# Four more of a gate stage's products come ahead of its second half, first pairs' weights are prepared on VectorE, and later pairs' sums queue behind the last operand

## The chip, the cores and the metric

One core of one Trainium2 chip runs the kernel. The metric is device time in microseconds (us), the median of three runs: 1529.71 us before the change (1528.55 to 1529.90). The page and the trace come from one more, profiled execution of the same program, which took 1530.54 us; its span from the first to the last instruction is 1528.7 us.

## The reference

One layer of a streaming encoder on 1024 tokens of width 1024, all in float32. The input is normalised and multiplied by `w_in` (1024 x 4256), whose columns hold a gated convolution (three times 512), the latents of an attention (384, 256 and 32) and two gates of 1024 columns each. After the attention and the output projection come an up-projection to 2 x 2816 columns, a width-3 convolution, gelu times value, a down-projection and a small gated embedding.

```
z = u @ w_in[i]
a_b, a_c, a_x, q_lat, kv_lat, k_rope, gate_a, gate_b = jnp.split(z, split_pts, axis=-1)
...
mixed = jax.nn.sigmoid(gate_a) * ya + jax.nn.sigmoid(gate_b) * yb
...
up = _causal_dwconv3(u2 @ w_ffn_up[i], conv_ffn_w[i]) + b_ffn_conv[i]
```

## The kernel before

**Products.** Every float32 matrix is held as a pair of parts, hi (ScalarE's cast, line 182) and lo (source minus hi, line 183, mostly VectorE or GpSimd), and a product of two matrices is three passes of four 128x512 matmuls: 12 matmuls (`prod`, line 306). Activations lie as eight 128x1024 tiles `u[0..7]`; the two 512-token halves are h = 0 and h = 1.

**Pairs.** Two 128-column blocks of a weight matrix are taken together. Their 2x2 block product is made with seven products instead of eight (`pair`): A11·B11, A12·B21, S2·T2, S3·T3, S1·T1, A22·T4, S4·B22. B11 and B21 come from half 0 of the activations (`first`), B22, T2, T3, T1 and T4 need half 1 as well (`second`, `third`; differences on VectorE over 128x2048, line 281, each operand then cast and split). S1 to S4 are sums and differences of the four weight blocks, made in `weights`: loads r1 and r0, the split of A22 (`who[1]`), a22 = a21 + a22 (line 336, `who[2]`), a21 = a11 - a21 (line 337, `who[3]`), and on VectorE lines 338 and 339 and two 128x1024 splits, S3 with S1 and S2 with S4. `who` is VectorE for the first and GpSimd for the other three by default. Evictions from PSUM are VectorE's lines 362, 365, 366, 375, 376, 377 and 381.

**First rows.** The products of A11 and A12 need half 0 alone. `first_row` loads a pair's first weight block a second time, splits it on VectorE and makes these two products ahead of time; ScalarE copies them out as m1 and d11 (lines 319, 324). The pair itself then has five products, its weights skip the split of A11 and A12 (`early`), and GpSimd adds m1 to d11 (line 364).

**The two places.** In the gate stage (column pairs 0 to 7 of the two gates) pairs 0 to 5 have first rows, made while half 1 is still being normalised; pairs 0 and 1 are spilled to DRAM (`d_z`) and reloaded when their turn comes, and pairs 6 and 7, made late in the stage ahead of the attention, have none. In the up-projection 12 of 22 pairs have first rows; the first pair in `order` has none, and its weights are all GpSimd's: `up_weights` passes `(G, G, G, G)`. In the down-projection, which the change does not touch, the first weights are VectorE's already.

**What sets the order.** A scheduler orders each engine's queue from the written program and its dependencies. `tc.issue_after(i)` puts the instructions written inside it behind `i` where they are on the engine of `i`, and does nothing to those on other engines. Each engine, and SyncE's DMA queue SP, works in order. Slots (s7, s8, s42, s43 for raw weights) are handed on when their last reader is done. TensorE's PSUM banks come from a ring of six in the gate stage and of four in the up-projection.

## Time and profile before

| | |
|---|---|
| median of three runs | 1529.71 us (1528.55 to 1529.90) |
| profiled execution | 1530.54 us, span 1528.7 us |
| TensorE busy | 1472.8 us (96%), mean granted clock 0.987 |
| VectorE busy | 1179.2 us (77%) |
| ScalarE busy | 698.6 us (46%) |
| GpSimd busy | 524.0 us (34%) |
| DMA | 195.56 MB, mean 128 GB/s |

The shares are averages over stages. TensorE is at 20.00 us of each 20 us window in most of the span; what is left are a few stretches in which it is not, and these are where a gain can lie. PE is TensorE, DVE VectorE, ACT ScalarE, POOL GpSimd, SP SyncE's queue.

### The profile page before, as it was taken

The page shows a single profiled execution, that of the slowest core. Times are in us where ns is not written, and L with a number is a line of the kernel's source. Part 1 is how long each engine was busy: PE and PEld are TensorE (multiplying, and loading weights), DVE is VectorE, ACT ScalarE, POOL GpSimd, SP SyncE. Part 2 cuts the span into 40 slices and gives each one's busy share as a digit, 9 for nine tenths or more (in the row PEclk, how much of TensorE's full clock was granted, in tenths as well). Part 3 has the DMA queues.
Part 4 walks back from the last instruction along what each step waited for, and adds up shares of the span by engine and source line. Part 5 has one row for each costly group of instructions (what it writes and reads, how often), then busy time and mean ns, then how long its engine had stood idle before and what let it go on. Part 6 is the DMA issues. An engine that isn't in the chain of part 4 may idle for free. (4 is left out here: it accounts for less than half of the span.)

```text
span 1528.7 us, 19246 instructions
## 1 busy us (share of the span) xinstructions
PE 1472.8 (96%) x6980; PEld 1226.6 (80%) x6980; DVE 1179.2 (77%) x1649; ACT 698.6 (46%) x1096; POOL 524.0 (34%) x388
## 2 busy tenths in 40 slices
PE   8989999999989999999997999999999999999896
PEld 6768888888768888888886888888888888787796
DVE  6898566665658888752668888999888889978886
ACT  8634222335447777443454434443434634334333
POOL 1424222215533443441127233344221021333953
PEclk9999999999999999999998999999999999999898
DMA  9325221335761012541380323433334552333432
GB/s 342 129 101 200 90 83 56 124 111 188 261 188 40 27 56 84 193 138 51 121 305 28 104 95 120 129 124 110 112 120 165 186 175 69 124 118 110 138 104 97
DMA packets 73503, 195.56 MB, mean 128 GB/s; under 512 B 7360, under 2 KB 22208, under 8 KB 73408
## 3 DMA queue, kind: packets, MB, share of 16 engines
q1 hardware_dynamic: 65056, 169.90, 34.2%
q10 hardware_dynamic: 8352, 24.44, 4.2%
q8 instruction: 55, 0.90, 0.3%
q14 instruction: 40, 0.33, 0.1%
HBM read 142.79 MB, written 51.51 MB: 127 GB/s over the span
## 5 line engine op out<-in xcount | busy, mean ns | idle before, releaser
L306 PE MATMUL psum<-s,s 128*128 128x512 f32 x3948 | 907.4, 391 | 18.5 <-DVE s L183 14.2
L306 PEld LDWEIGHTS psum<-s,s 128*128 128x128 f32 x3948 | 742.3, 189 | 178.3 <-DVE s L183 17.7
L182 ACT CAST s<-s 128x1024 fp32r<-128x1024 f32 (+3 forms) x419 | 337.3, 828 | 400.5 <-PE psum L306 137.9
L217 PE MATMUL psum<-s,s 128*128 128x512 f32 (+1 forms) x1920 | 416.6, 375 | 17.2 <-ACT s L182 11.5
L183 POOL TENSOR_TENSOR s<-s,s 128x512 fp32r<-128x512 f32 (+2 forms) x150 | 225.8, 1517 | 544.8 <-PE psum L306 352.5
L217 PEld LDWEIGHTS psum<-s,s 128*128 128x128 f32 x1920 | 336.5, 191 | 81.3 <-ACT s L182 14.0
L183 DVE TENSOR_TENSOR s<-s,s 128x1024 fp32r<-128x1024 f32 (+2 forms) x269 | 327.9, 1238 | 52.9 <-ACT s L182 43.2
L535 DVE SCALAR_TENSOR_TENSOR psum<-s,vecs,psum 128x1023 f32<-128x1023 f32 x88 | 111.7, 1279 | 2.5 <-ACT psum L533 1.5
L533 ACT ACTIVATE psum<-s,vecs 128x1024 f32<-128x1024 f32 x44 | 53.2, 1209 | 101.9 <-DVE s L377 88.1
L183 DVE TENSOR_TENSOR s<-psum,s 128x512 fp32r<-128x512 f32 (+3 forms) x144 | 70.8, 504 | 26.9 <-ACT s L182 25.8
L364 POOL TENSOR_TENSOR s<-s 128x512 f32<-128x512 f32 x22 | 33.5, 1523 | 158.1 <-DVE s L322 72.8
L182 ACT CAST s<-psum 128x512 fp32r<-128x512 f32 (+3 forms) x144 | 61.2, 445 | 38.5 <-DVE s L183 13.9
L753 PE MATMUL psum<-s,s 128*128 128x512 f32 (+2 forms) x288 | 67.4, 360 | 2.3 <-ACT s L764 2.1
L250 ACT ACTIVATE s<-s 128x512 f32<-128x512 f32 (+1 forms) x68 | 38.9, 581 | 63.5 <-DVE s L1061 29.9
L766 POOL TENSOR_SCALAR s<-s,ri 128x384 f32<-128x384 f32 (+5 forms) x48 | 41.4, 864 | 70.2 <-DVE ri L765 55.5
L337 POOL TENSOR_TENSOR s<-s,s 128x512 f32<-128x512 f32 x39 | 56.8, 1456 | 2.9
L253 DVE TENSOR_TENSOR s<-s,s 128x512 f32<-128x512 f32 (+1 forms) x55 | 46.0, 837 | 15.2 <-ACT s L250 13.6
L375 DVE TENSOR_TENSOR s<-s,psum 128x512 f32<-128x512 f32 x47 | 32.1, 682 | 31.5 <-PE psum L306 31.4
L336 POOL TENSOR_TENSOR s<-s 128x512 f32<-128x512 f32 x39 | 54.9, 1408 | 2.9
L778 PE MATMUL psum<-s,s 128*128 128x256 f32 x320 | 54.1, 292 | 1.5 <-DVE s L183 0.7
L753 PEld LDWEIGHTS psum<-s,s 128*128 128x128 f32 x288 | 46.4, 189 | 9.9 <-ACT s L764 5.3
L764 ACT ACTIVATE s<-psum,nm 128x128 f32<-128x128 f32 (+3 forms) x64 | 47.6, 746 | 14.3 <-DVE nm L762 9.0
(120 smaller groups left out, 1159.3 us busy)
## 6 DMA issues: line engine op xcount, KB each, us to landing
s<-in_w_up_dram SPq DMA_DIRECT2D x56, 512.0 KB, 3.7
s<-in_w_in_dram SPq DMA_DIRECT2D x40, 512.0 KB, 4.2
s<-in_w_down_dram SPq DMA_DIRECT2D x36, 512.0 KB, 3.7
d_f<-s SPq DMA_DIRECT2D x22, 512.0 KB, 2.6
s<-in_x_dram SPq DMA_DIRECT2D x32, 256.0 KB, 5.4
d_sg<-s ACTq DMA_DIRECT2D x16, 512.0 KB, 3.1
s<-d_sg SPq DMA_DIRECT2D x16, 512.0 KB, 4.3
s<-d_f SPq DMA_DIRECT2D x16, 512.0 KB, 6.7
```

The source lines that it names most:

```text
L182: A.copy(hi, src)
L183: last.append((eng or V).tensor_sub(lo, src, f(hi)))
L217: nc.tensor.matmul(out_ps, w[c // HALF][pw][:, c % HALF : c % HALF + P], X[k][half][px][:, cs], start=start and a == 0 and k == 0, stop=st ...
L253: V.tensor_add(acc, acc, sq)
L306: nc.tensor.matmul(pt, w[pw][:, k * P : (k + 1) * P], blk[k][px], start=a == 0 and k == 0, stop=a == 2 and k == 3,)
L336: who[2].tensor_add(a22, a21, a22)
L337: who[3].tensor_sub(a21, a11, a21)
L533: A.activation(dst, src, AF.Identity, bias=bias, scale=w2)
L535: V.scalar_tensor_tensor(dst[:, i:], src[:, : S - i], w, dst[:, i:], op0=ALU.mult, op1=ALU.add)
L753: nc.tensor.matmul(st_[:, lo_ : lo_ + w_], q[part_q][:, o : o + P], parts(K[hd, kh])[part_k][:, 0:w_], start=part_q == 0 and part_k == 0, ...
L764: A.activation(pr[:, 0:n], st_[:, 0:n], AF.Exp, bias=nm, accum_out=sm)
L778: nc.tensor.matmul(po[:, 0:256], vt[:, kt, :], t_[:, kk * 256 : (kk + 1) * 256], start=kt == 0 and part == 0, stop=kt == 2 * b + 1 and par ...
```

## The change

Pairs 6 and 7 of the gates get first rows too, made after those of pairs 0 and 1; all four are spilled and reloaded. The first pair of the gate stage (now named pair 2 in both versions) has all of its weight work on VectorE, as has the first pair of the up-projection, where `third` now also waits in the queue for that pair's last split. The weights of later pairs (for the gates: pairs 3, 4 and 5) are written inside `issue_after(behind)`, where `behind` is the last split of T4 on VectorE, so that their VectorE sums stand behind it. GpSimd's addition of m1 to d11 is put behind the same pair's a21, where GpSimd makes that.

```diff
@@ x_blocks / third
                 operand("T4", 4, 0)
+            return ends["T4"].ins
@@ weights
-        who[3].tensor_sub(a21, a11, a21)
+        w["S3 made"] = who[3].tensor_sub(a21, a11, a21)
@@ pair
-            G.tensor_add(d11, d11, m1)
+            with tc.issue_after(w["S3 made"].ins):
+                G.tensor_add(d11, d11, m1)
@@ the gate stage
-    def gate_weights(i, early=False):
-        return weights(w_in[17 + 2 * i], w_in[18 + 2 * i], raws, early)
+    def gate_weights(i, early=False, who=(V, G, G, G)):
+        return weights(w_in[17 + 2 * i], w_in[18 + 2 * i], raws, early, who)
...
-    early, spilled = [47, 48, 45, 49], 2
-    NE = len(early) + spilled
-    for i in range(NE):
-        o = f32(early[(i - NE) % len(early)])
+    early, spilled = [47, 48, 45, 49], (0, 1, 6, 7)
+    for n, i in enumerate([*spilled, *range(2, 6)]):
+        o = f32(early[n % 4])
         first_row(w_in[17 + 2 * i], B, raws, mm, o[:, hs(0)], o[:, hs(1)])
-        if i < spilled:
+        if i in spilled:
             nc.sync.dma_start(d_z[i], o)
     second()
-    w = gate_weights(spilled, True)
-    third(w)
+    w = gate_weights(2, True, (V, V, V, V))
+    behind = third(w)
     others = Ring([44, 46])
...
+    def spilled_pair(i, o, hooks=()):
+        nc.sync.dma_start(f32(o), d_z[i])
+        gate_pair(i, o, others(), True, hooks)
+
+    for n, i in enumerate(range(2, 6)):
+        if n:
+            with tc.issue_after(behind):
+                w = gate_weights(i, True)
+        gate_pair(i, early[n], others(), True, w=w)
+    for i in range(2):
+        spilled_pair(i, early[i])
...
-    for i in range(NE, 8):
-        gate_pair(i, outs(), outs(), hooks=(mixer_in, mixer_load) if i == 7 else ())
+    others = outs
+    for i in (6, 7):
+        spilled_pair(i, outs(), (mixer_in, mixer_load) if i == 7 else ())
@@ the up-projection
-        return weights(w_up[j], w_up[NFF + j], raws, j in rows, (G, G, G, G))
+        return weights(w_up[j], w_up[NFF + j], raws, j in rows, (G, G, G, G) if j != order[0] else (V, V, V, V))
...
-    third()
+    behind = third(w)
...
-        now = up(j, up_weights(j))
+        with tc.issue_after(behind):
+            w = up_weights(j)
+        now = up(j, w)
```

Lines of `weights` and `pair` move by one or two: 336 to 339 become 337 to 340, 362 and 364 to 366 become 363 and 366 to 368.

**VectorE, gate stage, from the second 128x2048 difference on.** Tiles: s38 and s34 are the activations, s17 is B22, s21 T2, s25 T3, s29 T1 and the s38 with the highest number T4; s7, s8, s42 and s43 are raw weights; other numbers are weight parts. Before (pair 2's weights are s42 and s43, pair 3's are s7 and s8):

```order
L281 TENSOR_TENSOR s38_96<-s34_102,s38_96 128x4x512
L339 TENSOR_TENSOR s42_90<-s42_90 128x512
L183 TENSOR_TENSOR s2_134<-s43_91,s1_127 128x1024
L281 TENSOR_TENSOR s34_102<-s34_102,s38_96 128x4x512
L183 TENSOR_TENSOR s0_124<-s42_90,s6_422 128x1024
L281 TENSOR_TENSOR s34_102<-s34_102 128x4x512
L183 TENSOR_TENSOR s21_119<-s34_102,s21_119 128x2x512
L338 TENSOR_TENSOR s7_88<-s8_89,s7_88 128x512
L183 TENSOR_TENSOR s21_119<-s34_102,s21_119 128x2x512
L183 TENSOR_TENSOR s25_564<-s38_96,s25_564 128x2x512 x2
L183 TENSOR_TENSOR s29_569<-s38_96,s29_569 128x2x512 x2
L339 TENSOR_TENSOR s7_88<-s7_88 128x512
```

Now (pair 2's weights are s7 and s8; the first row is the split of pair 5's first row, the second that of pair 2's A22):

```order
L183 TENSOR_TENSOR s1_127<-s43_91,s0_124 128x1024
L183 TENSOR_TENSOR s2_134<-s8_89,s2_134 128x512
L281 TENSOR_TENSOR s34_102<-s34_102,s38_96 128x4x512
L337 TENSOR_TENSOR s8_89<-s8_89 128x512
L281 TENSOR_TENSOR s34_102<-s34_102 128x4x512
L338 TENSOR_TENSOR s8_89<-s7_88,s8_89 128x512
L183 TENSOR_TENSOR s21_119<-s34_102,s21_119 128x2x512 x2
L339 TENSOR_TENSOR s7_88<-s8_89,s7_88 128x512
L183 TENSOR_TENSOR s4_390<-s8_89,s50_358 128x1024
L183 TENSOR_TENSOR s25_624<-s38_96,s25_624 128x2x512 x2
L183 TENSOR_TENSOR s29_629<-s38_96,s29_629 128x2x512 x2
L340 TENSOR_TENSOR s7_88<-s7_88 128x512
```

Pair 3's sums (lines 338 and 339 on s7) are gone from among the operands; they now follow T4. Pair 2's A22 and lines 337 and 338, which were GpSimd's, stand on VectorE between the differences. Pair 2's split of S3 with S1 has moved from among the differences to just ahead of T3, and that of S2 with S4 (the fifth row before) to behind T4. Three rows ahead of the piece stands the split of pair 4's first row, the second of the two splits that are new here.

**TensorE, gate stage, end of the first rows.** s9 is B11 and s13 B21. Before:

```order
L306 MATMUL psum_69<-s13_188,s50_357 128x512 x4
L306 MATMUL psum_69<-s13_188,s4_389 128x512 x4
L306 MATMUL psum_69<-s13_188,s50_357 128x512 x4
L306 MATMUL psum_69<-s25_564,s1_127 128x512 x4
L306 MATMUL psum_69<-s25_564,s2_134 128x512 x4
L306 MATMUL psum_69<-s29_569,s1_127 128x512 x4
L306 MATMUL psum_69<-s29_569,s2_134 128x512 x4
L306 MATMUL psum_69<-s21_119,s6_422 128x512 x2
L306 MATMUL psum_69<-s17_539,s6_422 128x512 x2
```

Now, after the row that stands third above in both versions:

```order
L307 MATMUL psum_69<-s9_183,s0_124 128x512 x4
L307 MATMUL psum_69<-s9_183,s1_127 128x512 x4
L307 MATMUL psum_69<-s9_183,s0_124 128x512 x4
L307 MATMUL psum_69<-s13_188,s0_124 128x512 x4
L307 MATMUL psum_69<-s13_188,s1_127 128x512 x4
L307 MATMUL psum_69<-s13_188,s0_124 128x512 x4
L307 MATMUL psum_69<-s25_624,s50_358 128x512 x4
L307 MATMUL psum_69<-s25_624,s4_390 128x512 x4
L307 MATMUL psum_69<-s25_624,s50_358 128x512 x4
```

In all, 48 matmuls on s9 and s13 have come in ahead of the first T3 product, and that product is made in one go, with T3's lo part in its third row; T1, T4 and only then T2 follow it.

**VectorE, up-projection, from the split of B22 on.** The first pair's weights are s42 and s43. Before:

```order
L183 TENSOR_TENSOR s17_539<-s34_102,s17_539 128x2x512 x2
L281 TENSOR_TENSOR s38_2477<-s34_102,s38_2477 128x4x512
L281 TENSOR_TENSOR s34_102<-s34_102,s38_2477 128x4x512
L338 TENSOR_TENSOR s42_4890<-s43_4891,s42_4890 128x512
L281 TENSOR_TENSOR s34_102<-s34_102 128x4x512
L339 TENSOR_TENSOR s42_4890<-s42_4890 128x512
L183 TENSOR_TENSOR s21_119<-s34_102,s21_119 128x2x512 x2
L183 TENSOR_TENSOR s25_564<-s38_2477,s25_564 128x2x512 x2
L183 TENSOR_TENSOR s29_569<-s38_2477,s29_569 128x2x512 x2
L183 TENSOR_TENSOR s0_124<-s43_4891,s6_422 128x1024
L183 TENSOR_TENSOR s50_5859<-s42_4890,s45_5858 128x1024
L183 TENSOR_TENSOR s38_6238<-s34_102,s38_6238 128x2x512 x2
```

Now:

```order
L281 TENSOR_TENSOR s38_2485<-s34_102,s38_2485 128x4x512
L337 TENSOR_TENSOR s43_4899<-s43_4899 128x512
L281 TENSOR_TENSOR s34_102<-s34_102,s38_2485 128x4x512
L338 TENSOR_TENSOR s43_4899<-s42_4898,s43_4899 128x512
L281 TENSOR_TENSOR s34_102<-s34_102 128x4x512
L339 TENSOR_TENSOR s42_4898<-s43_4899,s42_4898 128x512
L183 TENSOR_TENSOR s21_119<-s34_102,s21_119 128x2x512 x2
L340 TENSOR_TENSOR s42_4898<-s42_4898 128x512
L183 TENSOR_TENSOR s0_124<-s43_4899,s6_422 128x1024
L183 TENSOR_TENSOR s25_624<-s38_2485,s25_624 128x2x512 x2
L183 TENSOR_TENSOR s29_629<-s38_2485,s29_629 128x2x512 x2
L183 TENSOR_TENSOR s50_5867<-s42_4898,s45_5866 128x1024
```

The first pair's lines 337 and 338 are VectorE's now, and so are the splits of its A22 and of A11 with A12, which stand just above the piece; the split of S3 with S1 stands ahead of T3, not behind T1.

## Rows read from the trace of the kernel before

**Rows 1.** Part 1 of the page: busy time, share of the span and instructions of TensorE and VectorE.

```profile
PE 1472.8 (96%) x6980; PEld 1226.6 (80%) x6980; DVE 1179.2 (77%) x1649; ACT 698.6 (46%) x1096; POOL 524.0 (34%) x388
```

**Rows 2.** Windows of 20 us at the gate stage: from:to and its length, then busy time (and count) of PE, weight loads, DVE, ACT and POOL, granted clock, DMA share, GB/s.

```profile
60.00:80.00 20.00, 17.90 (x76) 13.56 (x75) 20.00 (x11) 10.85 (x16) 11.13 (x6) 1.00 0.19 52
80.00:100.00 20.00, 15.46 (x53) 11.13 (x54) 17.41 (x21) 6.90 (x9) 6.17 (x3) 0.83 0.18 57
100.00:120.00 20.00, 20.00 (x90) 16.57 (x89) 19.59 (x39) 6.14 (x9) 5.28 (x4) 1.00 0.55 206
```

**Rows 3.** The same columns at the start of the up-projection.

```profile
820.00:840.00 20.00, 10.90 (x44) 8.22 (x43) 19.34 (x12) 7.02 (x9) 12.47 (x7) 0.82 0.03 6
840.00:860.00 20.00, 20.00 (x83) 16.34 (x82) 17.43 (x21) 6.44 (x7) 6.28 (x4) 0.92 0.28 100
860.00:880.00 20.00, 20.00 (x90) 16.57 (x89) 16.85 (x19) 10.11 (x11) 3.89 (x3) 1.00 0.39 129
```

**Rows 4.** Timeline of TensorE, gate stage: start, length, line, operation, count, and in brackets the idle time ahead and what ended it.

```profile
46.96 28.37 PE L306 MATMUL psum<-s,s 128*128 128x512 f32 x123
76.96 2.47 PE L306 MATMUL psum<-s,s 128*128 128x512 f32 x8 [1.63 <-DVE s L183]
...
85.40 1.22 PE L306 MATMUL psum<-s,s 128*128 128x512 f32 x2 [1.49 <-DVE s L183]
87.78 210.88 PE L306 MATMUL psum<-s,s 128*128 128x512 f32 x920 [1.16 <-DVE s L365]
```

**Rows 5.** Timeline of VectorE, gate stage, same columns.

```profile
52.59 2.03 DVE L183 TENSOR_TENSOR s<-s,s 128x1024 fp32r<-128x1024 f32 x1
54.54 2.28 DVE L281 TENSOR_TENSOR s<-s 128x2048 f32<-128x2048 f32 x1
56.74 0.68 DVE L338 TENSOR_TENSOR s<-s,s 128x512 f32<-128x512 f32 x1
57.35 2.35 DVE L183 TENSOR_TENSOR s<-s,s 128x1024 fp32r<-128x1024 f32 x2
59.62 3.38 DVE L281 TENSOR_TENSOR s<-s,s 128x2048 f32<-128x2048 f32 x1
62.92 1.78 DVE L339 TENSOR_TENSOR s<-s 128x512 f32<-128x512 f32 x1
...
77.43 7.92 DVE L183 TENSOR_TENSOR s<-s,s 128x1024 fp32r<-128x1024 f32 x5
85.27 1.77 DVE L339 TENSOR_TENSOR s<-s 128x512 f32<-128x512 f32 x1
```

**Rows 6.** Timeline of GpSimd, gate stage: the first and the last two of the ten instructions that start between 52 and 87 us.

```profile
52.24 1.29 POOL L364 TENSOR_TENSOR s<-s 128x512 f32<-128x512 f32 x1 [0.92 <-ACT s L324]
...
82.12 2.14 POOL L336 TENSOR_TENSOR s<-s 128x512 f32<-128x512 f32 x1
84.34 2.14 POOL L337 TENSOR_TENSOR s<-s,s 128x512 f32<-128x512 f32 x1
```

**Rows 7.** Timeline of TensorE, start of the up-projection.

```profile
795.98 31.33 PE L306 MATMUL psum<-s,s 128*128 128x512 f32 x137
827.94 2.20 PE L306 MATMUL psum<-s,s 128*128 128x512 f32 x8 [0.64 <-ACT s L319]
838.60 61.58 PE L306 MATMUL psum<-s,s 128*128 128x512 f32 x261 [8.46 <-DVE s L183]
```

**Rows 8.** Timeline of VectorE, start of the up-projection.

```profile
803.41 1.22 DVE L183 TENSOR_TENSOR s<-s,s 128x1024 fp32r<-128x1024 f32 x1
804.55 2.29 DVE L281 TENSOR_TENSOR s<-s 128x2048 f32<-128x2048 f32 x1
806.75 2.36 DVE L183 TENSOR_TENSOR s<-s,s 128x1024 fp32r<-128x1024 f32 x2
809.02 5.59 DVE L281 TENSOR_TENSOR s<-s,s 128x2048 f32<-128x2048 f32 x2
820.65 1.77 DVE L338 TENSOR_TENSOR s<-s,s 128x512 f32<-128x512 f32 x1 [6.04 <-POOL s L337]
822.35 3.37 DVE L281 TENSOR_TENSOR s<-s 128x2048 f32<-128x2048 f32 x1
...
826.25 15.71 DVE L183 TENSOR_TENSOR s<-s,s 128x1024 fp32r<-128x1024 f32 x10
```

**Rows 9.** Timeline of GpSimd, start of the up-projection.

```profile
804.86 12.02 POOL L183 TENSOR_TENSOR s<-s,s 128x512 fp32r<-128x512 f32 x2 [19.63 <-PE psum L306]
816.83 1.30 POOL L336 TENSOR_TENSOR s<-s 128x512 f32<-128x512 f32 x1
818.07 1.30 POOL L364 TENSOR_TENSOR s<-s 128x512 f32<-128x512 f32 x1
819.33 1.29 POOL L337 TENSOR_TENSOR s<-s,s 128x512 f32<-128x512 f32 x1
...
828.48 2.38 POOL L183 TENSOR_TENSOR s<-s,s 128x512 fp32r<-128x512 f32 x1 [4.91 <-ACT s L182]
```

**Rows 10.** Windows of 20 us, columns as in rows 2, ahead of the attention.

```profile
400.00:420.00 20.00, 17.80 (x79) 14.42 (x78) 12.14 (x19) 5.76 (x15) 7.65 (x6) 1.00 0.83 255
420.00:440.00 20.00, 17.54 (x71) 14.04 (x71) 7.84 (x15) 5.06 (x11) 3.53 (x3) 0.92 0.89 269
```

**Rows 11.** Part 6 of the page: DMA issues, count, KB each, median us from issue to landing.

```profile
s<-in_w_in_dram SPq DMA_DIRECT2D x40, 512.0 KB, 4.2
```

More of the change, by code (lines that the diff above doesn't have):

```diff
@@ L458, in gate_pair @@
             A.dma_start(d_sg[2 * i + j], f32(o_))
-    early, spilled = [47, 48, 45, 49], 2
-    NE = len(early) + spilled
-    for i in range(NE):
-        o = f32(early[(i - NE) % len(early)])
+    early, spilled = [47, 48, 45, 49], (0, 1, 6, 7)
+    for n, i in enumerate([*spilled, *range(2, 6)]):
+        o = f32(early[n % 4])
         first_row(w_in[17 + 2 * i], B, raws, mm, o[:, hs(0)], o[:, hs(1)])
-        if i < spilled:
+        if i in spilled:
             nc.sync.dma_start(d_z[i], o)
     second()
-    w = gate_weights(spilled, True)
-    third(w)
+    w = gate_weights(2, True, (V, V, V, V))
+    behind = third(w)
     others = Ring([44, 46])
-    for n, i in enumerate([*range(spilled, NE), *range(spilled)]):
-        o = early[n % len(early)]
-        if n >= len(early):
-            nc.sync.dma_start(f32(o), d_z[i])
-        gate_pair(i, o, others(), True, w=w if n == 0 else None)
+    def spilled_pair(i, o, hooks=()):
[8 more added lines that the diff above has]
+        spilled_pair(i, early[i])
     def rotary_tables():
```

## The prediction, as put on record before the run

> **What bounds the kernel now.** I read the busy times first: TensorE works 1472.8 us of a span of 1528.7 [rows 1], so at most some 56 us can be had anywhere, and only where TensorE waits. Then the 20 us windows: nearly all show TensorE at 20.00 with 90 matmuls of 128x512, which is 20/90 = 0.222 us a matmul. Two places that the change touches do not. In the gate stage two windows hold 76 and 53 matmuls, 51 short of 180, so 51 x 0.222 = **11.3 us** are lost there [rows 2]. At the start of the up-projection two windows hold 44 and 83, 53 short, so **11.8 us** [rows 3]. In both the granted clock falls after the waits (0.83; 0.82, then 0.92), so part of the time ran at 1.2 GHz and not at 2.4; the matmul counts have that in them.
>
> Next, the timeline of TensorE for what ends the waits. In the gate stage it runs without a gap from 46.96 us for 123 matmuls, then stops and starts until 87.78 us, and VectorE's line 183, the splits, ends the waits [rows 4]. In the up-projection there is one wait of 8.46 us, ended by the same line [rows 7]. Then VectorE itself: from 52.59 to 87 us in the gate stage it has no idle time, 20.00 of 20 in one window [rows 2, 5]; in the up-projection it is busy too, but for 6.04 us in which its line 338 waits for GpSimd's line 337 [rows 8]. So the time of both places is set by how soon VectorE is through the differences and splits of half 1, and by how much TensorE has to do until then.
>
> **A price that both places need.** On VectorE alone a 128x1024 split takes 1.14 us from start to start (two in 57.35 to 59.62), a 128x2048 difference 2.2 (54.54 to 56.74) and a 128x512 sum 0.61 (56.74 to 57.35). The same three are also found at 2.03, 3.38 and 1.78 [rows 5]: 0.8 to 1.1 us more, each time with a GpSimd instruction under way. Ten of those start between 52 and 87 us [rows 6]. Taking 1.1 us each, they cost VectorE 11 us there; summed from its lone durations, the same stretch would be 10.6 us shorter. So in these stretches one GpSimd instruction costs VectorE about 1.1 us, almost twice the 0.61 of the sum that it spares it. The Trainium skill has a rule that speaks the other way (Perfetto Trace Analysis, section Optimizing Scalar/DVE Operations): where VectorE is saturated, handing work to ScalarE or even GpSimd may make sense; it adds that the shared SBUF port may undo this between VectorE and GpSimd. By the rule's first half the three sums taken over would make the operands 1.8 us later in each place; by the rows they come 1.5 us earlier (3 x 1.1 less 3 x 0.61). By the rule the sum would be 2 x 3.3 us higher; the rows decide, and the rule's case is rival (e).
>
> **Gate stage.** *Added to TensorE ahead of the operands:* the first rows of pairs 6 and 7, 48 matmuls, 10.7 us; pairs 6 and 7 have as many fewer, so TensorE's total is unchanged. Of the 123 matmuls from 46.96 us, 91 are first rows and 32 already pair 2's, by the order on TensorE. Now 139 come first: 46.96 + 139 x 0.222 = 77.8 us. T3's lo part is then wanted 8 matmuls on, at 79.6; T1's 20 on, at 82.2; T4's 32 on, at 84.9; the lo part of S2 44 on, at 87.6.
> *VectorE,* from 52.59 in the new order: up to the end of T3 it has eight splits of 1.14 us or pairs of halves that come to as much (the first rows of pairs 3, 4 and 5; B22 twice; T2 twice; S3 with S1), two more for T3, four differences of 2.2 and A22 and the three sums of 0.61: 10 x 1.14 + 4 x 2.2 + 4 x 0.61 = 22.6 us. T1 adds 2.3, line 340 0.6, T4 2.3, line 339 0.6 and S2 with S4 1.1. That gives T3 at 75.2, T1 at 77.5, T4 at 80.4 and S2 at 82.2. GpSimd has about five instructions left in this stretch (pair 3's three and two additions), up to 5.5 us: then T3 is at 79.6 (four of them by then), T1 at 83.0, T4 at 85.9 and S2 at 87.7. Against what TensorE wants, that is 0 to 1.0 us late. Behind it pair 2's evictions stand after pair 3's sums and splits, and pair 3's second product needs a bank that the first of them frees: up to 1.5 us more. I keep **2.0 us** of the 11.3 as waits and slow clock (bounds 0 and 6, the latter if GpSimd takes the ten turns that it has now): a gain of **9.3 us**.
> *What else is issued.* The two first rows load 512 KB each once more, two d_z stores are added, and two reloads: six transfers of about 4.2 us to landing [rows 11]. Four fall in a stretch with a DMA share of 0.19 and 0.18 [rows 2], and cost nothing while TensorE has first rows to do; without that cover a late weight block would hold VectorE (last rival). The splits of the two first rows only move forward on VectorE. ScalarE's copies of m1 and d11 and VectorE's line 362 go for pairs 6 and 7, ScalarE gets two copies each in the first rows, GpSimd one addition; they lie beside TensorE's full windows: 0. Putting the addition behind a21 on GpSimd moves it behind work that is due sooner: 0, with VectorE's line 367, which overwrites m1, next to wait if GpSimd is late.
>
> **Up-projection.** TensorE runs until 827.3 us as before, its order ahead of that being unchanged; now T3 with S3 comes first, and the lo part of S3 is wanted about 829 (8 matmuls on, as the x8 row ends about 830), T3's at 830, T1's at 833, T4's about 838 [rows 7]. *VectorE before:* two differences end at 814.6, then the 6.04 us for GpSimd, whose split of A11 with A12 and that of A22 took 12.02 us [rows 9]; then ten splits from 826.25, at 1.57 us each [rows 8]. *Now:* from 803.41 the splits of A11 with A12, A22, B22, T2 and S3 and the differences and sums up to the lo part of S3: with the last first row's split 7 x 1.14 + 4 x 2.2 + 5 x 0.61 = 19.8 us, which is 823.2. Four GpSimd instructions of the second pair may fall in, 4.4 us: 827.6, against 829 wanted. T3, T1 and T4 then come at 829.9, 832.2 and 836, in time. The next wait is for a PSUM bank: there are four, and pair one's fifth product needs the first eviction, which stands on VectorE behind T4 and the second pair's split, about 840 against 838.5. I keep **2.2 us** of 11.8 (bounds 0 and 8.5, the wait as it is): a gain of **9.6 us**.
>
> **Ahead of the attention** 30 matmuls, 6.7 us, are lost in two windows with a DMA share of 0.83 and 0.89 [rows 10]. The two reloads of 512 KB come shortly before, on the same SP queue as the convolution's and latents' loads, and pairs 6 and 7 take TensorE 10.7 us less to hide them. No row shows such a reload there; bounds: 3 us gained, if the shorter pairs free the operands' slots for those loads earlier, to 6.7 lost, if the stretch loses as much again. I take 0, since what ended those waits came after the gates.
>
> **Sum.** 1530.54 - 9.3 - 9.6 = 1511.6 for the profiled execution; the median of the runs shown is 0.8 lower, so **1511 us**.
>
> **The rivals.** (a) *One place only.* VectorE is late by what it was late before in one of the two: for it, VectorE keeps 19.59 of 20 us after the gap in the gate stage [rows 2], and 17.43 in the up-projection [rows 3]; against it, the counted operand times. 1529.7 less 9.3 or 9.6 gives **1520 to 1520.4**. (b) *Paid ahead of the attention.* The reloads delay the loads there and half of what is lost now is lost again, with 1 us of clock: **1515**. (c) *Nothing moves.* The wait goes from the operands to the evictions behind them, in both places in full; against it, six banks in the one and VectorE's order in both: **1529 to 1530**. (d) *Slower.* The weights of pair 2 arrive late. VectorE works in order, and A22's split now stands ahead of all T operands; its block is loaded on SP behind three d_z stores, each of which waits for a ScalarE copy. I expect the load to be issued about 54 us, when the slot is free, and landed at 58; VectorE comes to it at 62 to 63. Each us past that is a us in front of everything, and costs TensorE more: in the two windows of the gate stage 6.6 us without a matmul (20 less 17.90 and 20 less 15.46) went with 11.3 us lost, a factor of 1.7. It eats both gains from a landing at 63 + 18.9/1.7 = 74 us on; at 80 us the time is **1540**. For it, SP's strict order; against it, the idle DMA engines in that stretch.
>
> (e) *The sums spare VectorE nothing.* If the work taken over from GpSimd only adds its 0.61 us each and frees no turns, the operands come 3.3 us later than counted in each place: 1511 + 6.6 = **1517.6**; against it, all the long durations lie beside GpSimd's [rows 5, 6, 8, 9].
>
> **How the numbers follow.** Forecast 0.68, (a) 0.15, (b) 0.07, (e) 0.04, (c) 0.03, (d) 0.03. The forecast's own range is 1506.6 (both places closed in full, 23.1 us) to 1516 (their residues at 4 to 5 us each). The range takes in (a), (b) and (e): **1506 to 1521**. Differences under 0.2%, 3.1 us, can hardly be told from none. Faster: 0.94; same, which is (c): 0.03; slower, which is (d): 0.03.
>
> **What would show it.** Windows of 20 us with 86 to 90 matmuls and a granted clock of 1.00 around 80 to 100 us and around 810 to 830; VectorE's idle time at line 338 gone from the up-projection; its splits of the T operands nearer to 1.14 than to 1.57 us; about five and not ten GpSimd instructions among the gate's operands. Wrong would be a wait of over 4 us in either place, whichever engine ends it, VectorE idle ahead of A22's split on a w_in load, or over 40 matmuls missing ahead of the attention.

## The result, and the profile after

The changed kernel takes **1518.39 us** (median of five runs, 1517.30 to 1524.11) beside 1529.71 us for the kernel before (five runs, 1528.55 to 1532.69). The ratio is **0.9934, 95% interval 0.9919 to 0.9949**: 7.8 to 12.4 us faster. The forecast was 1511 us with a range of 1506 to 1521: the time lies inside that range, but outside the forecast's own, 1506.6 to 1516, and of the 18.7 us of gain only a little over half came.

The profiled execution took 1521.76 us, 3.4 us more than the median. Its busy times stand as in [rows 1]: TensorE does the same work, so the gain is waiting that went.

```profile
PE 1472.8 (97%) x6980; PEld 1227.8 (81%) x6980; DVE 1180.4 (78%) x1654; ACT 700.8 (46%) x1100; POOL 522.7 (34%) x383
```

The windows of 20 us at the two places and at the untouched ones, columns as in [rows 2]:

```profile
60.00:80.00 20.00, 20.00 (x90) 16.58 (x89) 17.22 (x13) 10.75 (x15) 11.52 (x4) 1.00 0.25 82
80.00:100.00 20.00, 18.27 (x72) 14.00 (x71) 19.26 (x31) 8.76 (x12) 6.89 (x5) 0.91 0.27 83
120.00:140.00 20.00, 19.69 (x87) 16.00 (x86) 14.16 (x16) 8.72 (x12) 8.79 (x7) 1.00 0.43 139
400.00:420.00 20.00, 19.44 (x86) 15.80 (x85) 8.54 (x18) 5.54 (x15) 3.56 (x3) 1.00 0.93 297
420.00:440.00 20.00, 17.85 (x75) 14.36 (x73) 8.52 (x14) 6.02 (x12) 7.10 (x6) 0.91 0.79 261
820.00:840.00 20.00, 14.31 (x59) 10.90 (x58) 13.44 (x13) 4.51 (x5) 14.32 (x7) 0.95 0.21 56
840.00:860.00 20.00, 20.00 (x80) 16.25 (x79) 16.37 (x19) 9.34 (x9) 7.87 (x5) 0.88 0.20 72
```

Counted as the prediction counts, 90 matmuls to a full window and 0.222 us each: in the gate stage (60 to 140 us) 18 + 3 = 21 are missing where 51 were [rows 2], a gain of 6.7 us. At the start of the up-projection (820 to 860) 31 + 10 = 41 are missing where 53 were [rows 3], a gain of only 2.7 us. Ahead of the attention two windows lack 19 matmuls where they lacked 30 [rows 10]; as that stretch now stands some 6 us earlier and two fixed windows cut another piece out of it, I go by checkpoints there. The first attention matmul came at 444.36 us and comes at 438.48, 5.9 us earlier, near the 6.7 of the gate stage: nothing is paid on the way. (In E1 and E3 below, the same program up to here, it comes at 435.68 and 437.20.) TensorE reaches the last transposes ahead of the up-projection at 789.99 instead of 795.62, 5.6 us earlier.

**Gate stage.** TensorE, to be laid beside [rows 4] (start, length, line, operation, count; in brackets the idle time ahead and what ended it):

```profile
46.96 36.77 PE L307 MATMUL psum<-s,s 128*128 128x512 f32 x161
84.83 0.73 PE L307 MATMUL psum<-s,s 128*128 128x512 f32 x2 [1.11 <-DVE s L183]
85.97 0.73 PE L307 MATMUL psum<-s,s 128*128 128x512 f32 x2 [0.41 <-ACT s L182]
```

It now runs 161 matmuls without a gap where it ran 123. At 83.7 us it stops for 1.11 us, until VectorE's last split of T1 is done (84.78), and then 0.41 and 0.21 us for ScalarE's casts of T4; it never waits for T4's splits. With 8 matmuls these 1.7 us are the smaller part of the 18 that window 80:100 lacks; the others went with the granted clock of 0.91. E8 below, with the same 1.7 us idle in that window at a clock of 1.00, has 80 matmuls there and not 72. VectorE, to be laid beside [rows 5]:

```profile
68.28 0.69 DVE L338 TENSOR_TENSOR s<-s,s 128x512 f32<-128x512 f32 x1
71.74 2.36 DVE L183 TENSOR_TENSOR s<-s,s 128x1024 fp32r<-128x1024 f32 x2 [2.78 <-ACT s L182]
...
74.62 10.16 DVE L183 TENSOR_TENSOR s<-s,s 128x1024 fp32r<-128x1024 f32 x5
...
85.95 2.36 DVE L183 TENSOR_TENSOR s<-s,s 128x1024 fp32r<-128x1024 f32 x2 [0.57 <-ACT s L182]
```

VectorE now waits for ScalarE's casts, 2.78 us for T2's and 0.57 for T4's. What held ScalarE is in its own timeline, and GpSimd's shows why:

```profile
70.14 0.63 ACT L459 ACTIVATE s<-s 128x512 f32<-128x512 f32 x1 [3.07 <-POOL s L366]
70.67 1.99 ACT L182 CAST s<-s 128x1024 fp32r<-128x1024 f32 x2
...
81.48 1.05 ACT L182 CAST s<-s 128x1024 fp32r<-128x1024 f32 x1 [4.80 <-POOL s L338]
...
84.87 2.94 ACT L182 CAST s<-s 128x1024 fp32r<-128x1024 f32 x3 [0.51 <-DVE s L183]
```

```profile
63.26 6.84 POOL L366 TENSOR_TENSOR s<-s 128x512 f32<-128x512 f32 x1 [43.81 <-ACT s L325]
75.16 1.83 POOL L183 TENSOR_TENSOR s<-s,s 128x512 fp32r<-128x512 f32 x1 [5.06 <-ACT s L182]
77.07 2.15 POOL L337 TENSOR_TENSOR s<-s 128x512 f32<-128x512 f32 x1
79.30 2.15 POOL L338 TENSOR_TENSOR s<-s,s 128x512 f32<-128x512 f32 x1
81.42 2.29 POOL L366 TENSOR_TENSOR s<-s 128x512 f32<-128x512 f32 x1
```

GpSimd's addition for pair 2 (line 366) takes 6.84 us where such an addition takes 1.29 [rows 6]: it ends at 70.10, just 1.1 us after VectorE has stopped at 68.97. A sigmoid of pair 2 (line 459) waits for it, and T2's two casts stand behind that sigmoid in ScalarE's queue. At 81.48 a cast for pair 3's S3 waits likewise for GpSimd's line 338, with T4's casts behind it; that costs nothing yet, since T4's casts (84.87) have to wait for VectorE's splits of T1 anyway, which end at 84.78.

**Up-projection.** TensorE, VectorE, GpSimd and ScalarE, to be laid beside [rows 7 to 9]; all of it stands 5.6 us earlier:

```profile
831.06 2.57 PE L307 MATMUL psum<-s,s 128*128 128x512 f32 x10 [0.21 <-ACT s L182]
838.81 51.43 PE L307 MATMUL psum<-s,s 128*128 128x512 f32 x213 [5.18 <-DVE s L367]
```

```profile
817.26 6.89 DVE L183 TENSOR_TENSOR s<-s,s 128x1024 fp32r<-128x1024 f32 x6
824.07 0.68 DVE L363 TENSOR_TENSOR s<-psum,s 128x512 f32<-128x512 f32 x1
830.10 2.36 DVE L183 TENSOR_TENSOR s<-s,s 128x1024 fp32r<-128x1024 f32 x2 [5.35 <-ACT s L182]
832.37 1.78 DVE L339 TENSOR_TENSOR s<-s,s 128x512 f32<-128x512 f32 x1
834.19 1.63 DVE L340 TENSOR_TENSOR s<-s 128x512 f32<-128x512 f32 x1
836.93 1.23 DVE L183 TENSOR_TENSOR s<-s,s 128x1024 fp32r<-128x1024 f32 x1 [1.11 <-ACT s L182]
838.08 0.68 DVE L367 TENSOR_TENSOR s<-psum,s 128x512 f32<-128x512 f32 x1
```

```profile
816.45 8.85 POOL L183 TENSOR_TENSOR s<-s,s 128x512 fp32r<-128x512 f32 x1 [35.12 <-PE psum L307]
...
826.75 1.29 POOL L338 TENSOR_TENSOR s<-s,s 128x512 f32<-128x512 f32 x1
```

```profile
828.07 3.46 ACT L182 CAST s<-s 128x1024 fp32r<-128x1024 f32 x4 [8.49 <-POOL s L338]
```

Read it from the bottom of the chain. TensorE waits 5.18 us for a PSUM bank, which VectorE's line 367 frees. That line is late since T4's splits (830.10) stand ahead of it and waited 5.35 us for T4's casts; the second pair's two sums (1.78 and 1.63 us, beside GpSimd) and a split that waits 1.11 us for its cast stand between. T4's casts are the second and third of the four at 828.07, whose first needs the second pair's a21 (line 338 on GpSimd). And a21 is late since GpSimd's split of the second pair's A22, begun at 816.45, took 8.85 us: it ended 1.2 us after VectorE's six back-to-back splits, which went at their lone pace (6 in 6.89 us). GpSimd did not slow VectorE here; VectorE shut GpSimd out.

### The profile page after: what moved, and what is told of

It reads as the page before. It is cut to its first block, busy times and chain, and to the rows that moved or that the text cites. A ratio compares the mean times of both kernels' runs of the same rounds, so it can differ in the third digit from the quotient of the medians.

```text
span 1520.0 us, 19261 instructions
## 1 busy us (share of the span) xinstructions
PE 1472.8 (97%) x6980; PEld 1227.8 (81%) x6980; DVE 1180.4 (78%) x1654; ACT 700.8 (46%) x1100; POOL 522.7 (34%) x383
## 5 line engine op out<-in xcount | busy, mean ns | idle before, releaser
L183 POOL TENSOR_TENSOR s<-s,s 128x512 fp32r<-128x512 f32 (+2 forms) x147 | 219.9, 1508 | 558.5 <-PE psum L307 337.2
L543 DVE SCALAR_TENSOR_TENSOR psum<-s,vecs,psum 128x1023 f32<-128x1023 f32 (+1 forms) x88 | 111.7, 1278 | 4.3 <-ACT psum L541 3.3
L366 POOL TENSOR_TENSOR s<-s 128x512 f32<-128x512 f32 x24 | 45.8, 1908 | 135.5 <-DVE s L323 80.5
L338 POOL TENSOR_TENSOR s<-s,s 128x512 f32<-128x512 f32 x37 | 52.8, 1428 | 2.9
L337 POOL TENSOR_TENSOR s<-s 128x512 f32<-128x512 f32 x37 | 51.0, 1378 | 2.9
L253 DVE TENSOR_TENSOR s<-s,psum 128x512 f32<-128x512 f32 x28 | 19.1, 685 | 41.1 <-ACT psum L250 40.4
```

Source lines behind the costliest of these rows:

```text
L183: last.append((eng or V).tensor_sub(lo, src, f(hi)))
L253: V.tensor_add(acc, acc, sq)
L337: who[2].tensor_add(a22, a21, a22)
L338: w["S3 made"] = who[3].tensor_sub(a21, a11, a21)
L543: V.scalar_tensor_tensor(dst[:, i:], src[:, : S - i], w, dst[:, i:], op0=ALU.mult, op1=ALU.add)
```

## The experiments

Each was timed beside the kernel before, in 4 to 12 executions. Missing matmuls are counted in the profiled execution over 60 to 140 us (of 360) and 820 to 860 us (of 180); before has 51 and 53. Each count is of one execution: E2, E6 and E7 have the change's up-projection, with the same 5.35 us wait for T4's casts, and lack 33, 35 and 35 where the change lacks 41.

| kernel | us (median) | ratio, 95% interval | missing, gate / up |
|---|---|---|---|
| the change | 1518.39 | 0.9934 (0.9919 to 0.9949) | 21 / 41 |
| E1 gate part and order line | 1516.77 | 0.9927 (0.9910 to 0.9943) | 21 / 29 |
| E2 up part and order line | 1522.69 | 0.9960 (0.9945 to 0.9975) | 51 / 33 |
| E5 order line alone | 1523.14 | 0.9957 (0.9940 to 0.9974) | 42 / 30 |
| E9 the change without order line | 1522.02 | 0.9965 (0.9953 to 0.9977) | 16 / 50 |
| E6 the change without new first rows | 1521.43 | 0.9950 (0.9932 to 0.9969) | 44 / 35 |
| E7 the change, pair 2 on GpSimd | 1525.75 | 0.9977 (0.9966 to 0.9988) | 51 / 35 |
| E3 ScalarE order, up-projection | 1511.99 | 0.9889 (0.9872 to 0.9906) | 20 / 9 |
| E4 E3 and ScalarE order, gates | 1514.63 | 0.9908 (0.9894 to 0.9922) | 23 / 8 |
| E8 E3 and additions of m1 on VectorE | 1513.01 | 0.9892 (0.9873 to 0.9910) | 17 / 9 |
| E10 E8 and a finer ScalarE order | 1508.97 | 0.9876 (0.9862 to 0.9889) | 9 / 12 |

The "order line" is the smallest edit of the diff, GpSimd's addition of m1 to d11 put behind the same pair's a21.

### The parts of the change: E1, E2, E5, E9

E1 takes the up-projection's part back:

```diff
-        ... (G, G, G, G) if j != order[0] else (V, V, V, V))
+        ... (G, G, G, G))
-    behind = third(w)
+    third()
-        with tc.issue_after(behind):
-            w = up_weights(j)
-        now = up(j, w)
+        now = up(j, up_weights(j))
```

> The gate stage as changed, the up-projection's first pair again with GpSimd's weights, T operands not queued behind them and later pairs' sums free. Theory (queues): of the 11.3 us that the gate stage lost before, the changed kernel still loses 4.7 by its windows, so this part alone is worth 5.9 to 6.6 us: 1523 to 1524. The up-projection shows the wait of 8 to 9 us that it had before, ended by VectorE's splits. Rival (one place only): the gate part carries the whole 11.3 us, 1518 to 1519, and the up-projection's part is worth nothing.

E2 is the kernel before with just these three edits the other way, and the order line.

> The gate stage as before (its additions on GpSimd put behind a21 as in the change), the up-projection as changed. Theory (queues): 2.7 us by the windows of the profiles (53 matmuls short before, 41 after): 1526 to 1528, with a wait of about 5 us for the first eviction, line 367. Rival (the two places add nothing to each other or VectorE's lead is eaten later): 1529 to 1530.

Neither came as the first theory had it: E1 was no slower than the whole change, and E2 gained 6 us where 3 were expected. The two gains add up to 17 us where both parts together gave 10. What they share is the order line, so E5 adds it alone to the kernel before (the diff below), and E9 takes it alone out of the change (its last two lines the other way):

```diff
-        who[3].tensor_sub(a21, a11, a21)
+        w["S3 made"] = who[3].tensor_sub(a21, a11, a21)
...
-            G.tensor_add(d11, d11, m1)
+            with tc.issue_after(w["S3 made"].ins):
+                G.tensor_add(d11, d11, m1)
```

> The kernel before with one line of the change: GpSimd's additions of m1 to d11 stand behind the same pair's a21. Theory: the run with the gate part alone lost only 6.4 us at the start of the up-projection where the kernel before loses 11.8, because this order alone takes GpSimd's additions out from among VectorE's splits of the T operands. So 4 to 6 us faster than before (1522 to 1524 us beside a before of 1528), about 61 and 90 matmuls in the windows 820:840 and 840:860, the gate stage still 50 matmuls short. Rival: the 6.4 us came with the gate part, which leaves the loads and queues ahead of the up-projection in another state; then this kernel is within 1.5 us of before and the up-projection still lacks some 50 matmuls.

> The changed kernel without the one line that puts GpSimd's additions of m1 to d11 behind the same pair's a21. Theory: that line is worth 4 to 6.6 us by itself (1523.1 beside a before of 1529.3), and the gate part about as much; without the line the changed kernel gives up 3 to 6 us and stands at a ratio of 0.995 to 0.998 to before. Rival: the line only matters where the first pair's weights are GpSimd's, since then its additions stand among the operands; with the first pairs on VectorE it is worth nothing and the ratio stays within 0.001 of 0.9934.

Both theories held, but that E5's gate stage lacks 42 matmuls and not 50. The line alone is worth 0.0043 of 1529 us, **6.6 us**, most of what the whole change gains; in the change it is worth 0.9965 - 0.9934 = 0.0031, 4.7 us, with an uncertainty of some 3 us in either figure. With the same uncertainty the rest follows: E5 to E1 is the gate part, 4.6 us; E5 to E2 and E1 to the change is the up-projection's part, 0.0003 and 0.0007 on the slow side, which is **no gain that can be seen**. What the line does in the kernel before, E5 shows in the up-projection, on VectorE, GpSimd and TensorE:

```profile
814.07 0.69 DVE L338 TENSOR_TENSOR s<-s,s 128x512 f32<-128x512 f32 x1 [6.17 <-POOL s L337]
...
819.68 10.30 DVE L183 TENSOR_TENSOR s<-s,s 128x1024 fp32r<-128x1024 f32 x9
```

```profile
822.46 8.68 POOL L183 TENSOR_TENSOR s<-s,s 128x512 fp32r<-128x512 f32 x1 [8.42 <-ACT s L182]
```

```profile
827.77 6.64 PE L306 MATMUL psum<-s,s 128*128 128x512 f32 x28 [1.50 <-DVE s L183]
837.44 12.80 PE L306 MATMUL psum<-s,s 128*128 128x512 f32 x49 [3.04 <-DVE s L362]
```

No addition stands between GpSimd's lines 336 and 337 any more, and the scheduler has moved VectorE's line 338 ahead of one of the differences: counted from the transposes at the stage's start (795.62 before, 792.77 here), line 338 comes 3.7 us earlier than in [rows 8]. Then nine splits take 10.30 us at lone pace where ten took 15.71 [rows 8], for the second pair's split on GpSimd is held beside them for 8.68 us and takes no turns. TensorE's wait of 8.46 us [rows 7] becomes 1.50 and 3.04: 23 matmuls, 5.1 us, come back here (24 in E1). What the line does in the change, E9 shows, on GpSimd and then on VectorE:

```profile
797.24 25.61 POOL L365 TENSOR_TENSOR s<-s 128x512 f32<-128x512 f32 x3 [20.82 <-ACT s L325]
```

```profile
812.31 6.89 DVE L183 TENSOR_TENSOR s<-s,s 128x1024 fp32r<-128x1024 f32 x6
819.12 0.68 DVE L363 TENSOR_TENSOR s<-psum,s 128x512 f32<-128x512 f32 x1
829.99 2.36 DVE L183 TENSOR_TENSOR s<-s,s 128x1024 fp32r<-128x1024 f32 x2 [10.18 <-ACT s L182]
```

Three additions that nobody waits for stand ahead of the second pair's split and a21, and take 25.61 us; three lone ones are 3 x 1.28 = 3.8, and counted back from their end at 822.85 they began at 819.0, when VectorE's run of splits was over. T4's wait doubles to 10.18 us. By the windows E9 differs from the change by 9 matmuls here and 5 the other way in the gate stage, 0.9 us in all, while the times differ by 4.7. These two profiles can't show the rest: E9's profiled execution, 1519.47 us, is the fastest of its runs and faster than the change's, 1521.76.

### The two terms of the gate stage: E6 and E7

E6 makes pairs 6 and 7 without first rows again; E7 gives pair 2's A22, a22 and a21 back to GpSimd.

```diff
# E6
-    early, spilled = [47, 48, 45, 49], (0, 1, 6, 7)
+    early, spilled = [47, 48, 45, 49], (0, 1)
...
-        o = f32(early[n % 4])
+        o = f32(early[(n - 2) % 4])
...
-        spilled_pair(i, outs(), (mixer_in, mixer_load) if i == 7 else ())
+        gate_pair(i, outs(), outs(), hooks=(mixer_in, mixer_load) if i == 7 else ())
# E7
-    w = gate_weights(2, True, (V, V, V, V))
+    w = gate_weights(2, True)
```

> The changed kernel without the first rows of pairs 6 and 7 (they are made late with seven products, as before); the rest of the change stays. Theory: the 48 matmuls are the cover. TensorE reaches the operands 10.7 us sooner and VectorE only 2.3 us sooner (two splits of 1.14), so the 4.7 us lost in the gate stage become 11 to 13: 6 to 8 us slower than the changed kernel, 1524 to 1526 us. Rival: VectorE's new order alone closed the gate stage; then within 2 us of the changed kernel, 1517 to 1520.

> The changed kernel with pair 2's weights in the gate stage made as before (the split of A22, a22 and a21 by GpSimd). Theory: GpSimd gets at its operands only where VectorE pauses, so pair 2's S3 and S1 come late, and VectorE's line 339 and the split of S3 with S1, which stand among the operands, wait for them: the gate stage loses 2 to 5 us more than the 4.7 of the changed kernel, 1520.5 to 1523.5. Rival by the count in the prediction (1.1 us for a GpSimd instruction against 0.61 of VectorE's): 1.5 us slower at most, 1518.5 to 1520. A second rival: VectorE is spared three instructions and GpSimd has time; then 1 to 2 us faster, 1516.5 to 1517.5.

E6 lands between its two theories: 0.0016 slower than the change, 2.4 us, within the uncertainty of both, so the times alone don't show that the first rows gain. By the windows they keep 23 matmuls, 5.1 us, from being lost in the gate stage, less than the 6.3 to 8.3 expected. E6's timeline of VectorE says why it is no simple difference of two start times:

```profile
75.75 10.43 DVE L183 TENSOR_TENSOR s<-s,s 128x1024 fp32r<-128x1024 f32 x9 [5.91 <-ACT s L182]
```

With two splits fewer, VectorE ran into ScalarE's queue for 5.91 us and then did nine splits at lone pace. E7 is clearer: 0.0043 slower, 6.6 us, more than expected; all 51 matmuls are missing again. VectorE in E7, then TensorE:

```profile
68.93 1.76 DVE L339 TENSOR_TENSOR s<-s,s 128x512 f32<-128x512 f32 x1 [3.92 <-POOL s L338]
...
73.42 15.90 DVE L183 TENSOR_TENSOR s<-s,s 128x1024 fp32r<-128x1024 f32 x10
```

```profile
86.98 28.20 PE L307 MATMUL psum<-s,s 128*128 128x512 f32 x116 [3.65 <-DVE s L183]
119.00 16.19 PE L307 MATMUL psum<-s,s 128*128 128x512 f32 x63 [3.82 <-DVE s L183]
```

VectorE waits 3.92 us for pair 2's a21, and its ten splits, T4's included, end at 89.3 us instead of 88.3; TensorE waits 3.65 us among them. Up to 100 us 25 matmuls are missing, 7 more than in the change; another 26, where the change lacks 3, go from 100 us on, with a second wait of 3.82 us for a later pair's split. So the weights on VectorE are worth at least as much as the first rows, though by the windows most of that is lost in the pairs that follow; what leads to the second wait was not traced.

### ScalarE's queue: E3, E4, E8, E10

If the chain above is right, the up-projection's wait goes when T4's casts no longer stand behind the second pair's. E3 remembers ScalarE's casts and writes later pairs' weights behind the last of T4's:

```diff
-        A.copy(hi, src)
+        casts.append(A.copy(hi, src))
...
     behind = third(w)
+    cast4 = casts[-1].ins
...
-        with tc.issue_after(behind):
+        with tc.issue_after(behind), tc.issue_after(cast4):
             w = up_weights(j)
```

> The changed kernel, with later pairs' ScalarE instructions in the up-projection's weights queued behind the cast of T4 (they stood ahead of it and waited for GpSimd's a21, which VectorE's splits had kept from SBUF). Theory (ScalarE's queue is the link): VectorE's wait of 5.35 us ahead of T4's split goes, line 367 follows T4's split at once, TensorE's wait of 5.18 us goes to under 1.5 and of the 41 matmuls missing 25 to 35 come back: 6 to 8 us, 1510 to 1512.5. Rival (VectorE's amount of work sets the time, not ScalarE's queue): the split of T4 comes earlier but the evictions no sooner, under 2 us gained, 1516 to 1518.5.

Met: 1511.99. The two windows of E3, and T4's splits on VectorE, now without a wait:

```profile
820.00:840.00 20.00, 20.00 (x90) 16.57 (x89) 15.82 (x16) 8.05 (x9) 13.27 (x8) 1.00 0.22 57
840.00:860.00 20.00, 18.65 (x81) 14.79 (x81) 18.77 (x22) 10.21 (x11) 5.46 (x4) 1.00 0.27 103
```

```profile
822.18 2.35 DVE L183 TENSOR_TENSOR s<-s,s 128x1024 fp32r<-128x1024 f32 x2
```

Against the change, 32 of the 41 missing matmuls are back, and the clock stays at 1.00. E4 does the same in the gate stage, with the sigmoids too:

```diff
-            with tc.issue_after(behind):
+            with tc.issue_after(behind), tc.issue_after(cast4):
                 w = gate_weights(i, True)
-        gate_pair(i, early[n], others(), True, w=w)
+        with tc.issue_after(cast4):
+            gate_pair(i, early[n], others(), True, w=w)
```

> As the one before, and in the gate stage too the later pairs' ScalarE casts and pairs 2 to 5's sigmoids are queued behind T4's cast; in the changed kernel a sigmoid that waited for a GpSimd addition of 6.84 us stood ahead of T2's casts and left VectorE idle for 2.78 us. Theory: the 2.78 us go, the operands come 2 to 3 us earlier, 10 to 18 of the gate's 21 missing matmuls come back, 2 to 4 us more than in the one before: 1507 to 1510. Rival (GpSimd's turns are what delays VectorE there): GpSimd's four instructions fall among the operands as before, and this gains under 1 us over the one before.

A miss: 2.6 us slower than E3. VectorE's 2.78 us wait went, and with it the pause that had let GpSimd in. GpSimd, ScalarE and TensorE in E4:

```profile
62.94 16.00 POOL L366 TENSOR_TENSOR s<-s 128x512 f32<-128x512 f32 x1 [43.83 <-ACT s L325]
83.51 1.30 POOL L183 TENSOR_TENSOR s<-s,s 128x512 fp32r<-128x512 f32 x1 [4.58 <-ACT s L182]
```

```profile
88.44 1.05 ACT L182 CAST s<-s 128x1024 fp32r<-128x1024 f32 x1 [4.04 <-POOL s L338]
```

```profile
93.27 1.20 PE L307 MATMUL psum<-s,s 128*128 128x512 f32 x4 [1.25 <-ACT s L182]
```

The same addition now takes 16.00 us and ends at 78.9. But GpSimd then waits 4.58 us more for ScalarE's cast of pair 3's A22, which E4 itself has put behind T4's; so pair 3's sums are late, and TensorE waits at 92 us instead of 84. E8 starts from E3 and gives the addition to VectorE wherever VectorE makes a21:

```diff
+        w["adder"] = who[3]
...
-                G.tensor_add(d11, d11, m1)
+                w["adder"].tensor_add(d11, d11, m1)
```

> The best run so far (weights of later pairs in the up-projection also behind T4's cast on ScalarE, 1512.0) and, in the gate stage, the addition of m1 to d11 for pair 2 on VectorE in place of GpSimd. Theory: this addition took GpSimd 6.84 us because VectorE worked back to back; the sigmoid that needs it held up T2's casts on ScalarE, for which VectorE waited 2.78 us. On VectorE it costs 0.61 and the wait goes: the operands come 2 us sooner, and of the 21 matmuls that the gate stage lacks 8 to 14 come back: 1509 to 1510.5. Rival: the wait moves on to T4, whose casts stand on ScalarE behind a cast for pair 3 that waits for GpSimd's line 338; then within 1 us of that run, 1511 to 1513.

That is pair 2's addition, but also the eight of the down-projection, whose weights are all VectorE's (GpSimd has 374 instructions in E8, 383 in E3, VectorE nine more). They change little: from the last transposes ahead of the up-projection to the first behind the down-projection TensorE takes 589.2 us in E3, 589.8 in E8 and 588.7 in E10, which has the edit too.

The rival held: no gain over E3. T2 to T1 went through at lone pace, but VectorE then stood 6.94 us before T4's splits, whose casts were still behind pair 3's on ScalarE:

```profile
85.39 2.36 DVE L183 TENSOR_TENSOR s<-s,s 128x1024 fp32r<-128x1024 f32 x2 [6.94 <-ACT s L182]
```

E10 puts into E8 the other half, for pairs 3 to 5: their sigmoids, and of their casts that of S3 with S1 alone, behind T4's.

```diff
-        w["S3"], w["S1"] = wide(r1, V)
+        with tc.issue_after(tail or w["S3 made"].ins):
+            w["S3"], w["S1"] = wide(r1, V)
...
-                w = gate_weights(i, True)
-        gate_pair(i, early[n], others(), True, w=w)
+                w = gate_weights(i, True, tail=cast4)
+        with tc.issue_after(cast4 if n else behind):
+            gate_pair(i, early[n], others(), True, w=w)
```

> The best kernel so far with pair 2's addition on VectorE (1513.0; ratio 0.9892) and, in the gate stage, the ScalarE cast of S3 with S1 of pairs 3, 4 and 5 and these pairs' sigmoids behind T4's casts; the cast of A22 stays where it is. Theory: VectorE's 6.94 us wait for T4's casts went with ScalarE's queue, where they stand behind a cast and a sigmoid of pair 3 that need GpSimd. Now T4's split follows at 80 to 82 us, ahead of the 84.9 at which TensorE wants it: the 10 matmuls that window 80:100 lacks come back, and 1.5 to 3 us with them: ratio 0.987 to 0.9882, 1509 to 1511 beside a before of 1529. Rival: the wait moves on to pair 3's S3, whose a21 GpSimd makes while VectorE leaves it no room, as in the run with all of pair 3's casts behind T4's: then no gain, ratio 0.989 to 0.991.

The theory held; at 1508.97 us this is the fastest version, 18.9 us below before. TensorE in E10 does not stop in the gate stage until 123.7 us:

```profile
46.50 77.23 PE L307 MATMUL psum<-s,s 128*128 128x512 f32 x335
```

The interval of E10 (0.9862 to 0.9889) overlaps those of E8 and E3, so its lead over these is not clear from the times; that all three beat the change (0.9919 at the least) is.

## Why the prediction was right or wrong

**What bounds the kernel: right.** All that was gained came from the two places, TensorE's work stayed the same, and E10 shows that they hold what was forecast: 42 + 41 matmuls back, 18.4 us by the windows and 18.9 by the times, against the 18.9 of the two terms. That the change itself got 10 is a matter of three steps. And that its time fell inside the stated range was luck: the range reached to 1521 for the rivals' sake, and the order line, which the prediction priced at nothing, made up part of what the up-projection did not give. Without it (E9) the time is 1522.02 us, and by the ratio 1524 beside a before of 1529.71: outside.

**The addition behind a21, "0": wrong, and the largest miss.** It is worth 4.7 to 6.6 us (E9, E5). The prediction asked who waits for the addition (nobody early) and not what stands behind it on GpSimd: the a21 of the pair that comes next, for which ScalarE and VectorE wait. The row was there: in [rows 9] an addition stands at 818.07 between lines 336 and 337, while VectorE's line 338 waits [rows 8]. In E5, without it there, line 338 comes 3.7 us sooner.

**The price of 1.1 us for a GpSimd instruction: right in the one place, wrong in the other.** In the gate stage it holds to the second digit: five splits with four GpSimd instructions beside them take 10.16 us, 4.5 over five lone ones of 1.14. In the up-projection the four instructions that the step allowed for, 4.4 us, did not fall in. VectorE went at lone pace, and GpSimd was held up instead. The price was read from stretches in which the two take turns [rows 5], and the other case was in [rows 9] too: 12.02 us for two splits beside a VectorE that did not rest until 814.6.

**Up-projection, 9.6 us: the term that failed.** 2.7 us by the windows (4.0 to 4.4 in E2, E6 and E7), and beside the order line the edit itself gave no gain that can be seen (E2 against E5). Moved by the 5.6 us of the shift, T1 was forecast for 826.6 and was through by 824.1, earlier. But T4 was counted as VectorE's work alone; its casts were not looked up on ScalarE, where they stand behind a cast that hangs on GpSimd. Moved alike, T4 was forecast for 830.4 and ends at 832.5, and line 367 for 834.4 and ends at 838.8; half of that lateness is T4's, the rest that of the second pair's sums and split behind it. The wait that the prediction named, the bank for the fifth product, is the one that came; it was sized at 1.5 us (840 against 838.5) and is 5.18, and the granted clock fell to 0.95 and 0.88 behind it. The sign by which the forecast would be wrong, a wait of over 4 us, was met here. E3 confirms the cause: with ScalarE's order alone altered, 7.1 us come back by the windows and 6.9 by the ratios.

**Gate stage, 9.3 us: right in mechanism, 6.7 by the windows.** The residue was kept at 2.0 us and is 4.7. T1 was forecast for 83.0 and ends at 84.8, T4 for 85.9 and 88.3; behind that is the wait at 71.74, 2.78 us, which is again ScalarE's queue behind GpSimd. The forecast put T1 0.8 us late and it is 1.1, and the wait for a bank did not come; the largest part of the residue, 2.2 us, is the slow clock behind the short waits. Of the two means, the 48 matmuls and the weights on VectorE, the prediction priced the second at 1.5 us of earlier operands; E7 puts it at 6.6 us of time, and the 1.5 us were a reason but not the size. Whether the order line has a share here is open: E5 lacks 42 matmuls in this stage, and E2, with the same gate stage, 51.

**Ahead of the attention, 0, and the six transfers: right.** The checkpoints show no loss, VectorE never waits for a w_in load in the gate stage, and so rival (d) did not come about. Rival (a), one place only, is nearest to what happened in its time of 1520 and in its picture, since the up-projection kept most of its wait. Rival (e) is contradicted by E7, which gives pair 2's three instructions back to GpSimd and loses 6.6 us. The rule by which a saturated VectorE hands work over (the Trainium skill, Perfetto Trace Analysis, section Optimizing Scalar/DVE Operations) is not borne out here: E7 hands work back to GpSimd and loses 6.6 us, some 3 us either way. What the same passage adds, that the shared port may undo such a step between VectorE and GpSimd, agrees with these runs.

## What to carry to other kernels

Before an edit is priced at nothing because nobody waits for the moved instruction, look at what stands behind it in its queue, and follow that chain across engines: here VectorE shut GpSimd out, ScalarE stood behind GpSimd, VectorE behind ScalarE and TensorE behind VectorE. A recorded length many times the lone one was each time a wait here; look for the engine whose pause ends it. When a change has several parts, time the smallest one alone: it was most of the gain.

## What the runs showed of the hardware

The lockout of GpSimd was not expected at this size. A 128x512 instruction of 1.3 us took 8.85 us in the change and 16.00 in E4, ending 1.1 to 1.2 us after VectorE's run of two-input instructions had stopped (77.8 in E4) or come to one that reads PSUM (line 363 at 824.07); three took 25.61 in E9 and end three lone lengths after such a place (819.12). VectorE lost nothing meanwhile. In other stretches the two take turns, at 2.15 us for GpSimd's instruction and 1.1 us more for VectorE's. What decides between the two these rows don't show: at 75.16 in the change GpSimd got a turn though VectorE had been at work since 71.74 without a visible pause, and in E8 a split begun at 73.17 was held for 6.43 us. The Trainium skill (SBUF — State Buffer, section SBUF: two separate sides) has the shared port pair as an exclusive lock for a whole instruction, taken by the one that starts first; on VectorE's side it names instructions in a two-port mode or with two SBUF inputs. The rows agree, as far as GpSimd went on beside line 363, which reads one input from PSUM. But here GpSimd was kept out from one VectorE instruction to the next, for over 20 us in E9; why it gets no turn between them no run shows.

In stages that the change leaves alone, single profiled executions differ by some 3 us. E1 and the change are the same program up to the up-projection and stand level, within 0.03 us, at the transposes of 353.6 us. The first window in which they differ by more than one matmul is this one, here in E1:

```profile
420.00:440.00 20.00, 18.84 (x87) 15.36 (x86) 9.76 (x21) 6.68 (x13) 8.38 (x7) 1.00 0.78 261
```

The change has 75 matmuls there, at a granted clock of 0.91 and not 1.00, as shown above: twelve fewer, 2.7 us. That is most of the 3.4 us by which the change's profiled execution lies above its median.
